# A second level of seven products inside an MLP's first matrix product, for two of the outer seven

## The chip, the cores and the metric

The kernel runs on one core of one Trainium2 chip. The metric is the device time of one execution in microseconds. Before the change three runs gave 2006.57, 2002.11 and 2002.98 us, so the median is 2002.98 us. All arithmetic is in float32: each product of two matrices is made of three passes over operands that are split into a high and a low part.

## The reference, cut to what matters

The network has two layers: attention and an MLP, then a gated linear recurrence and an MLP. The change concerns the first matrix of both MLPs, `h @ w_up`:

```
def sqrelu_mlp(h, w_up, w_down):
    return jnp.square(jax.nn.relu(h @ w_up)) @ w_down
...
    h = rmsnorm(x, mlp_norm[layer])              # x: 1024 tokens x 1024
    x = x + sqrelu_mlp(h, mlp_w_up[layer], mlp_w_down[layer])   # w_up: 1024 x 4096
```

## The kernel before, in words

The hidden layer is made transposed: 4096 rows (hidden features, in 32 blocks of 128) by 1024 columns (tokens). Row block `m` and row block `m + 16` are done together; the kernel calls that a pair (`pair`, line 643), and there are 16 of them in each layer. A pair is a 2x2 block product: two row blocks, two halves of the 1024 inner features, two halves of the tokens (512 each). It is done with seven block products in place of eight (Strassen-Winograd). The seven are numbered 1 to 7. Product 2 multiplies the upper row block's second half of the features (its right weight block, as it is stored) by those features of the first 512 tokens; product 4 multiplies the lower row block's right weight block by a combination of token blocks. The other five have sums of weight blocks or the left ones.

One product (`product`, line 623) has 128 rows, 512 inner features and 512 columns: four blocks of 128 features, and for each of them three matmuls of 512 columns (`mm3`, line 431: high by high, high by low, low by high). So a product is 12 matmuls, a pair is 84, and each matmul has its own load of a 128x128 weight.

Around the products a pair does this:

- four weight tiles of 256 KB are loaded (`raw`, tag `wr`); four sums `s1` to `s4` are made on VectorE (DVE, tag `m`); each of the seven weights is split (`weight_split`, line 450) into a high part (`wh`, a copy on ScalarE, ACT, or on DVE) and a low part (`wl`, a subtraction on DVE);
- the products gather in three PSUM banks: `main` (tag `q`: 1, 6, 7, 4 on top of each other), `side` (`q`: 5 and 3) and `own` (tag `p`: 2). `main` is copied out after 1, after 6 and after 7 (tag `t`); `own` and `side` are added on DVE;
- the four blocks of the hidden layer are squared after a ReLU on ACT, and they and three differences of them are stored to DRAM (7 stores of 256 KB, `d<-t`), for the MLP's second product (`down`), which loads them again.

Ahead of the pairs, `finish` (line 561) makes the token blocks of the seven products with their splits.

Nothing is issued in the order of the code. Every operation is recorded with a cost, its engine or engines and its buffers (`Schedule.add`), and a planner (`due`, `order`) then sets the order on each engine: work is ranked by when the matrix engine will want it, and among what is ready the lowest rank goes first. Buffers are given out tag by tag in the order of recording; there are 20 of `t`, 7 of `m`, 5 each of `wr`, `wh`, `wl`, 4 PSUM banks each of `p` and `q`. All loads and stores stand in one queue, that of SyncE (SP), in the planned order. Since one helper issues everything, every instruction stands under one line of the profile (L372), and groups are told apart by their tiles' names.

Of the kernel before, what the change touches and what calls it, by code (L numbers as in the profile page):

```python
# [22 lines left out]
NH = 2  # L23
TH = T // NH
FF = 4096
MT = FF // P
# [16 lines left out]
CH = 64  # L43
LEVELS = 6
WARM = 10
K_SPANS = ((-1, 3), (2, 6), (5, 8))


# [88 lines left out]
LEAD = 100  # L137
# [3 lines left out]
HK = KT // 2  # L141
# [167 lines left out]
def straight(z):  # L309

    return z.rearrange("p (b a) -> p a b", a=2)


def halves(z):

    return z.rearrange("p (a b) -> p a b", a=2)


class Net:
# [241 lines left out]
    def finish(self, which, r=None):  # L561

        x, t, q01, q11 = self.b, [], [], []

        def stored(j):
            z = self.t()
            self.dma(z, self.u[j], 4 * P * TH)
            return z

        def lower():  # L570
            for j in range(HK):
                q01.append(self.gained(which, j, 1, r))
# [24 lines left out]
        yield  # L597
        for j in range(HK):
            z = stored(j + HK)
            self.tt("any", z, z, t[j], ALU.subtract)  # L600
            x[4].append(self.split(z))
        yield

    def mlp_first(self, layer):
        self.layer, self.hid, self.y = layer, {}, {}
        self.begin(2 + layer)
        self.weigh(0)

    def mlp_second(self):
# [5 lines left out]
    def take(self, out, bank):  # L615

        self.copy(halves(out), straight(bank))
# [5 lines left out]
    def product(self, ps, w, x, start, n=TH):  # L623
        more = {} if start else {"skip_group_check": True}
        for j in range(HK):
            c = slice(j * P, j * P + P)
            self.mm3(ps, (w[0][:, c], w[1][:, c]), x[j], start and j == 0, j == HK - 1, n, **more)
# [12 lines left out]
        self.s.lead = 0  # L640
        return w

    def pair(self, m, x):

        w = self.strassen_weights(*(self.io["up"][self.layer, i] for i in (m, m + MT // 2)))

        def read(ps):
            z = self.t()
            self.take(z, ps)
            return z  # L650

        main, side, own = self.psum("q"), self.psum("q"), self.psum()
        got = {}
        for name in (1, 5, 6, 2, 7, 3, 4) if m == MT // 2 - 1 else (1, 2, 5, 6, 3, 7, 4):
            ps = main if name in (1, 6, 7, 4) else own if name == 2 else side
            self.product(ps, w[name], x[name], name in (1, 2, 5))
            if name in (1, 5, 6, 7):
                got[name] = read(ps)
        u1, p5, u2, u3 = (got[name] for name in (1, 5, 6, 7))

        def kept(name, z):
            self.hid[name, m] = self.keep(z)

        self.add_bank(u1, own)
        h00 = self.square_relu(u1)
        kept(1, h00)
        self.add_bank(u2, side)
        h01, t5, t6, t4 = self.square_relu(u2), *(self.t() for _ in range(3))
        self.tt("any", t5, h01, h00, ALU.subtract)
        kept(5, t5)  # L670
        self.tt("any", p5, p5, u3, ALU.add)
        h11 = self.square_relu(p5)
        kept(3, h11)
        self.tt("any", t6, h11, t5, ALU.subtract)
        kept(6, t6)
        self.tt("any", h01, h11, h01, ALU.subtract)
        kept(7, h01)
        h10 = self.square_relu(main, True)
        kept(2, h10)
        self.tt("any", t4, h10, t6, ALU.subtract)  # L680
        kept(4, t4)

    def mlp(self, cut):

        x = self.mlp_second()
        for m in range(MT // 2):
            if m == MT // 2 - 2:
                self.r = [self.a() for _ in range(NH)]
                for hf in range(NH):
                    self.copy(self.r[hf], self.spread(self.square[hf]))  # L690
            if m == 1 and self.layer == 0:
                self.hgrn_constants()
            self.pair(m, x)
        yield from self.down(cut)

    def hidden(self, name, p):
# [879 lines left out]
```

## Time and profile before

| | |
|---|---|
| median of three runs | 2002.98 us |
| the profiled execution | 2004.15 us |
| its span in the profile | 2002.0 us (2.15 us lie around it) |
| busy, share of the span: PE, weight loads, DVE, ACT | 99%, 86%, 85%, 51% |
| DMA | 345.88 MB, mean 173 GB/s |
| granted TensorE clock | full (0.998) |

PE stands for the matrix engine's matmuls, PEld for its weight loads. A matmul's row holds the time from its start to its modelled end, and the next one starts before that end; so the pace of the engine is read from the starts of following rows, not from the mean duration. The same holds for DVE to a smaller degree. The first products of the MLP run from about 295 to 583 us in the first layer and from about 1378 to 1668 us in the second.

### The profile page before, as it was taken

To read this page: it belongs to the slowest core of one execution; us is meant where nothing else is said; L and a number is where in the kernel's file an instruction comes from. 1 tells how busy PE (TensorE), PEld (TensorE's weight loads), DVE (VectorE), ACT (ScalarE), POOL (GpSimd) and SP (SyncE) were. 2 spreads that over 40 slices of the span, in tenths; PEclk is the share of its full clock that TensorE was granted. 3 is DMA by queue.
4 is the path that set the end of the run, shared out by engine and by line. 5 is a ranking of instruction groups with operands and counts; after the bars stand their busy time and mean duration, and the time that the engine had idled before them with its cause. 6 is when DMAs were issued, how large, how long until landed. Compare 5 with 4: busy or idle time off the path is not lost.

```text
span 2002.0 us, 32707 instructions
## 1 busy us (share of the span) xinstructions
PE 1979.2 (99%) x11404; PEld 1721.3 (86%) x11404; DVE 1700.5 (85%) x3360; ACT 1011.1 (51%) x2045; POOL 61.2 (3%) x124
## 2 busy tenths in 40 slices
PE   9999999999999999999999999999999999999998
PEld 8877788888888888888888888888888888888887
DVE  8999899777779878799888999889977778887787
ACT  6566796554444323255345555553654445333352
POOL 4030000000000000000000000000000000000001
PEclk9999999999999999999999999999999999999999
DMA  6211463544469877745412212667444447896752
GB/s 217 90 53 59 126 221 122 184 165 160 149 200 302 293 231 260 238 163 176 151 59 80 80 59 85 210 200 246 150 158 158 155 165 236 282 308 216 236 179 85
DMA packets 196677, 345.88 MB, mean 173 GB/s; under 512 B 21536, under 2 KB 31776, under 8 KB 196512
## 3 DMA queue, kind: packets, MB, share of 16 engines
q1 hardware_dynamic: 195936, 343.28, 52.3%
q8 instruction: 89, 1.46, 0.3%
q14 instruction: 76, 0.62, 0.1%
q10 hardware_dynamic: 576, 0.52, 0.1%
HBM read 250.39 MB, written 93.32 MB: 172 GB/s over the span
## 4 chain that ended last, share of the span: by engine, by line
PE 84%; DVE 8%; DMA 3%; issue 2%; ACT 2%; SPq 0%; POOL 0%; POOLq 0%; DVEq 0%; ACTq 0%
PE q L372 50%; PE p L372 33%; DVE t L372 3%; DVE a L372 2%; DVE wl L372 1%; DMA t<-d 1%; ACT t L372 1%; ACT a L372 1%; DMA wr<-in_down 1%; DVE m L372 0%; DMA a<-in_x 0%; ACT wh L372 0%; DMA wr<-in_wqkv 0%; ACT m L372 0%; DMA wr<-in_wv 0%
## 5 line engine op out<-in xcount | busy, mean ns | idle before, releaser
L372 PE MATMUL q<-a,wh 128*128 128x512 f32 x2560 | 762.3, 380 | 1.4 <-ACT t L372 1.4
L372 PE MATMUL p<-a,wh 128*128 128x512 f32 x2112 | 645.1, 384 | 0.1
L372 PEld LDWEIGHTS q<-a,wh 128*128 128x128 f32 x2560 | 483.5, 189 | 70.6 <-ACT t L372 2.5
L372 PE MATMUL q<-a,wl 128*128 128x512 f32 x1280 | 485.4, 380 | 0.0
L372 PEld LDWEIGHTS p<-a,wh 128*128 128x128 f32 x2112 | 395.0, 190 | 53.9 <-issue 1.2
L372 PE MATMUL p<-a,wl 128*128 128x512 f32 x1056 | 402.1, 381 | 0.0
L372 ACT CAST a<-t 128x512 fp32r<-128x512 f32 x277 | 168.4, 619 | 294.7 <-PE q L372 141.2
L372 PEld LDWEIGHTS q<-a,wl 128*128 128x128 f32 x1280 | 242.4, 189 | 33.8
L372 ACT ACTIVATE t<-t 128x512 f32<-128x512 f32 x272 | 171.1, 631 | 184.0 <-DVE t L372 175.3
L372 DVE TENSOR_TENSOR wl<-wr,wh 128x512 fp32r<-128x512 f32 x352 | 241.5, 689 | 12.4 <-ACT wh L372 3.9
L372 DVE TENSOR_TENSOR t<-t,t 128x512 f32<-128x512 f32 (+3 forms) x364 | 225.7, 642 | 26.8 <-ACT t L372 23.3
L372 PEld LDWEIGHTS p<-a,wl 128*128 128x128 f32 x1056 | 200.2, 190 | 26.5 <-issue 0.4
L372 DVE TENSOR_TENSOR a<-t,a 128x512 fp32r<-128x512 f32 (+1 forms) x326 | 217.3, 689 | 2.9 <-ACT a L372 2.4
L372 DVE TENSOR_TENSOR wl<-m,wh 128x512 fp32r<-128x512 f32 x248 | 170.9, 691 | 18.0 <-ACT wh L372 10.6
L372 ACT COPY t<-q 128x512 f32<-128x512 f32 (+2 forms) x214 | 119.2, 560 | 112.1 <-PE q L372 111.0
L372 ACT CAST wh<-wr 128x512 fp32r<-128x512 f32 x175 | 107.6, 618 | 93.7 <-PE p L372 41.6
L372 DVE TENSOR_TENSOR m<-wr,wr 128x512 f32<-128x512 f32 x160 | 110.3, 691 | 41.9 <-DMA wr<-in_down 25.9
L372 DVE CAST wh<-wr 128x512 fp32r<-128x512 f32 x177 | 75.8, 428 | 79.7 <-PE q L372 47.1
L372 ACT CAST wh<-m 128x512 fp32r<-128x512 f32 x158 | 97.3, 618 | 56.6 <-PE q L372 34.8
L372 PE MATMUL p<-wh,a 128*128 128x512 f32 x352 | 111.0, 385 | 0.0
L372 PEld LDWEIGHTS q<-t,t 128*64 128x64 f32 (+1 forms) x2160 | 95.2, 144 | 13.7 <-issue 5.6
L372 PE MATMUL q<-t,t 128*64 128x32 f32 (+2 forms) x2160 | 104.1, 229 | 1.6 <-DVE t L372 1.3
(130 smaller groups left out, 2059.9 us busy)
## 6 DMA issues: line engine op xcount, KB each, us to landing
d<-t SPq DMA_DIRECT2D x276, 256.0 KB, 2.8
t<-d SPq DMA_DIRECT2D x264, 256.0 KB, 4.6
wr<-in_down SPq DMA_DIRECT2D x256, 256.0 KB, 4.0
wr<-in_up SPq DMA_DIRECT2D x128, 256.0 KB, 2.9
a<-d SPq DMA_DIRECT2D x60, 256.0 KB, 4.8
wr<-in_wqkv SPq DMA_DIRECT2D x48, 256.0 KB, 2.9
d<-a SPq DMA_DIRECT2D x48, 256.0 KB, 3.5
wr<-in_win SPq DMA_DIRECT2D x48, 256.0 KB, 3.0
```

The source lines that it names most:

```text
L372: fn(*[place(a) for a in args], **{k: place(v) for k, v in kw.items()})
```

## The change

For the pairs from number 4 on (`m > AT` with `AT = 2`), the pairs are taken in couples of two neighbours, `m` and `m + 1`: six couples in each layer. For a couple, product 2 of both pairs and product 4 of both pairs are made together. The two upper right weight blocks, stacked, are 256 rows by 512 features, and the token block is 512 by 512; that is again a 2x2 block product, of quarters: 128 rows, 256 features, 256 columns. `inner` does it with seven products of six matmuls with 256 columns each. Pairs 0 to 3 of each layer keep the seven outer products as they were.

```
+INNER = (2, 4)
+AT = 2
...
+    def inner(self, name, m, x):
...
+        a0, a1 = (self.raw(self.io["up"][self.layer, i + row * (MT // 2)][:, TH:]) for i in (m, m + 1))
+        sa, sb = self.t(tag="m"), self.t(tag="m")
...
+        self.tt("any", s1, a1[:, near], a1[:, far], ALU.add, half)
+        self.tt("any", s2, s1, a0[:, near], ALU.subtract, half)
+        self.tt("any", s3, a0[:, near], a1[:, near], ALU.subtract, half)
+        self.tt("any", s4, a0[:, far], s2, ALU.subtract, half)
+        wide = [self.weight_split(z) for z in (a0, sa, sb)]
+        hi, lo = (self.tile(tag, BUFS[tag], (P, TH), F32R) for tag in ("wh", "wl"))
+        self.copy(hi[:, far], a1[:, far], half, ("ACT", "DVE"), False)
+        self.tt("any", lo[:, far], a1[:, far], hi[:, far].bitcast(F32), ALU.subtract, half)
...
+        banks = [self.psum(), self.psum()]
+        main, side, own = banks[0][:, near].only(0), banks[1][:, near].only(0), banks[1][:, far].only(1)
+
+        def product(k, ps, start):
...
+            if k in made:
+                right = [self.t(F32R) for _ in range(2)]
+                for z, kept in zip(right, made[k]):
+                    self.dma(z.bitcast(F32), kept, 4 * P * TH)
+            for i in range(2):
...
+                self.mm3(ps, (wh, wl), (xh, xl), start and i == 0, i == 1, half, slice(0, half), **more)
...
+        product(1, main, True)
+        take(part[0, 0], main)
+        product(2, own, True)
+        add(part[0, 0], own)
+        product(6, main, False)
+        take(part[0, 1], main)
+        product(5, side, True)
+        product(7, main, False)
+        take(part[1, 1], main)
+        add(part[1, 1], side)
+        product(3, side, False)
+        add(part[0, 1], side)
+        product(4, main, False)
+        take(part[1, 0], main)
```

The token side of the inner products 5, 6, 7 and 4 is made once in a layer, by `prepare`: differences of quarters of the stored token blocks, split and stored to DRAM as eight tiles of 256 KB for each of the two names. It is recorded between the outer products of pair 2. `inner` loads them again, two tiles for each of the four products.

```
+    def prepare(self, name):
...
+        u = [self.t() for _ in range(HK)]
+        for z, kept in zip(u, self.quarters[name]):
+            self.dma(z, kept, 4 * P * TH)
+        yield
...
+        def stored(k, t):
+            made[k] = [self.keep(z.bitcast(F32)) for z in self.split(t.rearrange("p i c -> p (i c)"), self.t)]
...
+        difference(t1, low(far), low(near))
+        stored(5, t1)
+        yield
...
```

In `pair` the weights of the products in `done` are not split (their raw tiles are still loaded, since `s1` and `s4` need them), the products are left out, and their results come from `inner`:

```
-        for name in (1, 5, 6, 2, 7, 3, 4) if m == MT // 2 - 1 else (1, 2, 5, 6, 3, 7, 4):
+            if name in done:
+                if name == 4:
+                    late = done[4]()
+                continue
...
+            if name == 1 and 2 in done:
+                self.add_bank(done[2], main)
...
-        h10 = self.square_relu(main, True)
+        if 4 in done:
+            self.tt("any", late, late, u3, ALU.add)
+            h10 = self.square_relu(late)
+        else:
+            h10 = self.square_relu(main, True)
```

How the instructions stand now is shown at three places of the first layer. On PE before, this is the start of product 2 of pair 7: its bank is `p1360`, the token blocks are `a814` and so on, and the weight is `wh1348`, `wl1349`.

```order
L372 MATMUL p1360_5419<-a814_3642,wh1348_5336 128x512
L372 MATMUL p1360_5419<-a815_3702,wh1348_5336 128x512
L372 MATMUL p1360_5419<-a814_3642,wl1349_5344 128x512
L372 MATMUL p1360_5419<-a818_3675,wh1348_5336 128x512
L372 MATMUL p1360_5419<-a819_3735,wh1348_5336 128x512
L372 MATMUL p1360_5419<-a818_3675,wl1349_5344 128x512
```

On PE now, this is inner product 6 of name 4 for the couple of pairs 6 and 7 (bank `p1438`), and the start of inner product 5 (bank `p1439`); `t1442` to `t1445` are prepared token quarters that were loaded again, and `q1482` is the `main` bank of pair 7.

```order
L374 MATMUL p1438_5584<-t1442_5647,wh1432_5582 128x256
L374 MATMUL p1438_5584<-t1443_5656,wh1432_5582 128x256
L374 MATMUL p1438_5584<-t1442_5647,wl1433_5602 128x256
L374 MATMUL p1438_5584<-t1442_5647,wh1432_5582 128x256
L374 MATMUL p1438_5584<-t1443_5656,wh1432_5582 128x256
L374 MATMUL p1438_5584<-t1442_5647,wl1433_5602 128x256
L374 MATMUL q1482_5675<-a798_3259,wl1473_5678 128x512
L374 MATMUL p1439_5588<-t1444_5682,wh1432_5582 128x256
L374 MATMUL q1482_5675<-a802_3624,wh1472_5667 128x512
L374 MATMUL q1482_5675<-a803_3658,wh1472_5667 128x512
L374 MATMUL q1482_5675<-a802_3624,wl1473_5678 128x512
L374 MATMUL p1439_5588<-t1445_5689,wh1432_5582 128x256
```

A product of twelve matmuls with 512 columns in one run has become runs of six with 256 columns, and outer products of the couple stand between them. In all, 1008 matmuls of 256 columns (24 inner blocks of 42) have taken the place of 576 of 512 columns (24 times two products of 12).

On the SP queue before, this is the stretch of one pair: four weight tiles (`wr<-in_up`) and seven stores (`d<-t`).

```order
L372 DMA wr1552_5988<-in_up 128x512
L372 DMA d14941495_5994<-t1494_5982 128x512
L372 DMA wr1553_6008<-in_up 128x512
L372 DMA wr1554_6052<-in_up 128x512
L372 DMA d14991500_6066<-t1497_6057 128x512
L372 DMA wr1594_6091<-in_up 128x512
L372 DMA d15011502_6098<-t1501_6080 128x512
L372 DMA d15021503_6109<-t1498_6095 128x512
L372 DMA d15031504_6121<-t1496_6046 128x512
L372 DMA d15051506_6133<-t1505_6107 128x512
L372 DMA d15061507_6141<-t1499_6127 128x512
```

On the SP queue now, this is the end of a pair's stores and the loads for the inner block of the PE rows above.

```order
L374 DMA d13771378_5627<-t1370_5614 128x512
L374 DMA wr1465_5636<-in_up 128x512
L374 DMA t1442_5647<-d11771178_4712 128x512
L374 DMA t1443_5656<-d11781179_4720 128x512
L374 DMA t1446_5664<-d11881189_4796 128x512
L374 DMA t1447_5673<-d11891190_4810 128x512
L374 DMA t1444_5682<-d11661167_4655 128x512
L374 DMA t1445_5689<-d11671168_4664 128x512
L374 DMA wr1501_5698<-in_up 128x512
L374 DMA wr1502_5709<-in_up 128x512
L374 DMA t1448_5722<-d11961197_4829 128x512
L374 DMA t1449_5730<-d11971198_4843 128x512
```

Eight loads of prepared tiles and two more weight tiles for each inner block now stand between the stores and loads of the pairs: for a couple, 42 transfers of 256 KB where there were 22.

On DVE now, this is the work for the weights of the same inner block (`m1428` and `m1429` hold the four sums, 256 columns each), between the additions of the pair before and the reading of inner banks (`p`). Before, none of the rows with 256 columns was there, and a right weight block needed only its split.

```order
L374 TENSOR_TENSOR m1428_5531<-wr1427_5484 128x256
L374 TENSOR_TENSOR m1429_5538<-wr1426_5474,wr1427_5484 128x256
L374 TENSOR_TENSOR t1393_5458<-p1392_5447,t1393_5458 128x256
L374 TENSOR_TENSOR wl1418_5550<-m1410_5414,wh1417_5528 128x512
L374 TENSOR_TENSOR wl1420_5556<-m1409_5409,wh1419_5542 128x512
L374 TENSOR_TENSOR m1428_5531<-m1428_5531,wr1426_5474 128x256
L374 TENSOR_TENSOR t1369_5572<-t1372_5494,t1368_5452 128x512
L374 TENSOR_TENSOR wl1431_5576<-wr1426_5474,wh1430_5563 128x512
L374 TENSOR_TENSOR m1429_5538<-wr1426_5474,m1428_5531 128x256
```

The sums and splits of an inner block now stand among the last additions of the pair ahead of it and the readings of the inner block before.

## Rows read from the trace of the kernel before

**Rows 1.** The page: span, engines' busy time, granted clock, chain by engine.
```profile
span 2002.0 us, 32707 instructions
PE 1979.2 (99%) x11404; PEld 1721.3 (86%) x11404; DVE 1700.5 (85%) x3360; ACT 1011.1 (51%) x2045; POOL 61.2 (3%) x124
...
PEclk9999999999999999999999999999999999999999
...
PE 84%; DVE 8%; DMA 3%; issue 2%; ACT 2%; SPq 0%; POOL 0%; POOLq 0%; DVEq 0%; ACTq 0%
```
**Rows 2.** The chain in order of time, first layer's pairs: start, length, what.
```profile
444.12 2.59 PE p L372 x12
446.71 15.54 PE q L372 x72
462.25 2.59 PE p L372 x12
```
**Rows 3.** Stages of the first products: busy time by engine, clock, DMA share, GB/s.
```profile
295.00:331.00 36.00, 35.41 (x168) 30.86 (x167) 35.62 (x62) 25.66 (x47) 0.36 (x2) 1.00 0.39 130
331.00:367.00 36.00, 36.00 (x169) 31.59 (x168) 34.07 (x89) 23.70 (x43) 0.00 (x0) 1.00 0.56 187
367.00:583.00 216.00, 216.00 (x1010) 189.33 (x1009) 156.51 (x261) 103.93 (x178) 0.00 (x0) 1.00 0.47 160
1378.00:1414.00 36.00, 36.00 (x172) 31.50 (x171) 34.90 (x61) 22.98 (x41) 0.00 (x0) 1.00 0.49 154
1414.00:1450.00 36.00, 36.00 (x168) 31.57 (x167) 34.25 (x63) 21.98 (x42) 0.00 (x0) 1.00 0.53 176
1450.00:1666.00 216.00, 216.00 (x1010) 189.37 (x1010) 158.23 (x263) 105.46 (x180) 0.00 (x0) 1.00 0.46 159
```
**Rows 4.** Timeline of PE and PEld near the end: 512 columns, then 256.
```profile
1954.63 0.38 PE L372 MATMUL p<-a,wl 128*128 128x512 f32 x1
...
1963.70 0.38 PE L372 MATMUL p<-a,wl 128*128 128x512 f32 x1
...
1970.93 9.23 PEld L372 LDWEIGHTS p<-a,a 128*128 128x128 f32 x82
1970.95 9.40 PE L372 MATMUL p<-a,a 128*128 128x256 f32 x82
```
**Rows 5.** The page's groups: weight loads of the first products.
```profile
L372 PEld LDWEIGHTS q<-a,wh 128*128 128x128 f32 x2560 | 483.5, 189 | 70.6 <-ACT t L372 2.5
```
**Rows 6.** Stages of the second product (down), columns as in Rows 3.
```profile
583.00:619.00 36.00, 34.63 (x161) 29.98 (x160) 31.09 (x54) 20.37 (x36) 0.00 (x0) 1.00 0.87 286
640.00:710.00 70.00, 70.00 (x326) 61.43 (x325) 59.16 (x107) 23.45 (x40) 0.00 (x0) 1.00 0.90 301
700.00:710.00 10.00, 10.00 (x48) 8.79 (x47) 9.27 (x19) 2.48 (x4) 0.00 (x0) 1.00 0.98 343
```
**Rows 7.** Timeline of DVE: runs of 512 and of 256 columns.
```profile
442.26 1.29 DVE L372 TENSOR_TENSOR t<-t,t 128x512 f32<-128x512 f32 x2
...
1028.70 2.90 DVE L372 TENSOR_TENSOR t<-t,m 128x256 f32<-128x256 f32 x8
```
**Rows 8.** Groups on DVE, 367 to 583 us: busy, mean ns, idle before.
```profile
L372 DVE TENSOR_TENSOR wl<-m,wh 128x512 fp32r<-128x512 f32 x48 | 33.2, 691 | 5.1 <-ACT wh L372 3.5
L372 DVE CAST wh<-wr 128x512 fp32r<-128x512 f32 x35 | 14.9, 427 | 19.6 <-PE q L372 13.7 <-PE p L372 5.7
```
**Rows 9.** Timeline of PE: the wait of the first pairs.
```profile
317.34 1.05 PE L372 MATMUL q<-c,t 128*128 128x1 f32 x8 [0.59 <-DVE t L372]
```
**Rows 10.** The page's DMA issues: count, KB, median us to landing.
```profile
d<-t SPq DMA_DIRECT2D x276, 256.0 KB, 2.8
t<-d SPq DMA_DIRECT2D x264, 256.0 KB, 4.6
wr<-in_up SPq DMA_DIRECT2D x128, 256.0 KB, 2.9
```

More of the change, by code (lines that the diff above doesn't have):

```diff
@@ L601, in finish @@
             x[4].append(self.split(z))
+            if r is None and 4 in INNER:
+                self.quarters[4].append(self.keep(z))
         yield
@@ L606, in mlp_first @@
         self.begin(2 + layer)
+        self.quarters = {2: self.u[HK:], 4: []}
         self.weigh(0)
@@ L641, in strassen_weights, with difference @@
         return w
-    def pair(self, m, x):
-        w = self.strassen_weights(*(self.io["up"][self.layer, i] for i in (m, m + MT // 2)))
+    def prepare(self, name):
+        near, far = slice(0, TH // 2), slice(TH // 2, TH)
+        u = [self.t() for _ in range(HK)]
+        for z, kept in zip(u, self.quarters[name]):
+            self.dma(z, kept, 4 * P * TH)
+        yield
+        made = self.quarters[name] = {}
+        def difference(out, x, y):
+            for i in range(2):
+                self.tt("any", out[:, i].only(i), x(i), y(i), ALU.subtract, TH // 2)
+        def stored(k, t):
+            made[k] = [self.keep(z.bitcast(F32)) for z in self.split(t.rearrange("p i c -> p (i c)"), self.t)]
+        low, high = (lambda c: lambda i: u[i][:, c]), (lambda c: lambda i: u[2 + i][:, c])
+        new = lambda: self.t(F32, (P, 2, TH // 2))
+        part = lambda t: lambda i: t[:, i].only(i)
+        t1 = new()
+        difference(t1, low(far), low(near))
+        stored(5, t1)
+        yield
+        t2 = new()
+        difference(t2, high(far), part(t1))
+        stored(6, t2)
+        yield
+        t3 = new()
+        difference(t3, high(far), low(far))
+        stored(7, t3)
+        yield
+        difference(t1, high(near), part(t2))
+        stored(4, t1)
+        yield
@@ L647, in read, with pair @@
+    def pair(self, m, x, done, between=()):
+        w = self.strassen_weights(*(self.io["up"][self.layer, i] for i in (m, m + MT // 2)), done)
         def read(ps):
@@ L650, in read @@
             return z
-        main, side, own = self.psum("q"), self.psum("q"), self.psum()
+        main, side, own = self.psum("q"), self.psum("q"), None if 2 in done else self.psum()
         got = {}
         for name in (1, 5, 6, 2, 7, 3, 4) if m == MT // 2 - 1 else (1, 2, 5, 6, 3, 7, 4):
+            if name in done:
+                if name == 4:
+                    late = done[4]()
+                continue
             ps = main if name in (1, 6, 7, 4) else own if name == 2 else side
             self.product(ps, w[name], x[name], name in (1, 2, 5))
-            if name in (1, 5, 6, 7):
+            if name == 1 and 2 in done:
+                self.add_bank(done[2], main)
+            elif name in (1, 5, 6, 7):
                 got[name] = read(ps)
-        u1, p5, u2, u3 = (got[name] for name in (1, 5, 6, 7))
+            for steps in between:
+                next(steps, None)
+        p5, u2, u3 = (got[name] for name in (5, 6, 7))
         def kept(name, z):
             self.hid[name, m] = self.keep(z)
-        self.add_bank(u1, own)
+        u1 = done[2] if 2 in done else got[1]
+        if 2 not in done:
+            self.add_bank(u1, own)
         h00 = self.square_relu(u1)
@@ L677, in pair @@
         kept(7, h01)
-        h10 = self.square_relu(main, True)
+        if 4 in done:
+            self.tt("any", late, late, u3, ALU.add)
+            h10 = self.square_relu(late)
+        else:
+            h10 = self.square_relu(main, True)
         kept(2, h10)
@@ L685, in mlp @@
         x = self.mlp_second()
[L686 to L693, printed above, removed]
+        steps = [self.prepare(name) for name in INNER]
+        for m in range(0, MT // 2, 2):
+            done = {}
+            if m > AT:
+                done = {name: self.inner_of(name, m, x) for name in INNER}
+            for i in range(2):
+                if m + i == MT // 2 - 2:
+                    self.r = [self.a() for _ in range(NH)]
+                    for hf in range(NH):
+                        self.copy(self.r[hf], self.spread(self.square[hf]))
+                if m + i == 1 and self.layer == 0:
+                    self.hgrn_constants()
+                self.pair(m + i, x, {name: y(i) if name == 2 else lambda y=y: y(i) for name, y in done.items()}, steps if m + i == AT else ())
         yield from self.down(cut)
```

30 lines of the change are left out of this document (added).

## The prediction

> **What bounds the kernel now.** I read the page's head first: PE is busy 99% of 2002.0 us, at the full clock in all 40 slices, and the chain that ended last lies on PE for 84% [rows 1]. Next, the chain inside the first layer's first products: 2.59 us of twelve matmuls in bank `p` (product 2), 15.54 us of seventy-two in `q` (the other six), then `p` again [rows 2]. So a pair takes 462.25 - 444.12 = 18.13 us, a couple 36.26 us, and the chain names nothing but PE there. Third, the stages of the first products: from 331 to 583 us and from 1378 to 1666 us PE is busy for the whole of each stretch; only the first 36 us lose 0.59 [rows 3], to one wait for DVE [rows 9]. DVE is nearly full in the first two couples of a layer (34.07 to 35.62 of 36 us) and has 26.1 us of work in each of the later six (156.51 / 6); ACT 17.3 us (103.93 / 6); DMA moves 160 GB/s at a share of 0.47. Here PE's matmuls set the time, one for one, and the question is what else becomes full when they get fewer.
>
> **The matmuls.** The pace is read from starts. With 512 columns, 14 rounds of three begin between 1954.63 and 1963.70: 9.07 / 42 = 0.216 us each. With 256 columns and a weight load for each matmul, as in `inner`, 82 loads take 9.23 us; less the last one's 0.19 [rows 5] that is 9.04 / 81 = 0.112 us each, and the matmuls beside them keep that pace (82 in 9.40 us) [rows 4]. Half the columns cost 52% of the time, not half: the load of 128 weight columns, hidden behind 512 columns, is just about the pace with 256. An inner block has 42 matmuls: 42 x 0.112 = 4.70 us. The two outer products that it replaces have 24: 24 x 0.216 = 5.18 us. It saves 0.48 us, and there are 2 names x 6 couples x 2 layers = 24 blocks: **-11.5 us**. A couple shrinks to 36.26 - 0.96 = 35.3 us.
>
> The Trainium skill speaks against this: "TensorE: Matmul & The Clock Gate", Part 3, "The mechanism", says that a weight load overlaps a running matmul only when the two use different row groups. All loads here use all 128 rows, so by that rule each of the 1008 loads would stand alone; at the 0.19 us of rows 5 the change would cost up to 1008 x 0.19 = 192 us. The rows disagree: 82 loads and 82 matmuls of 256 columns go by in the same 9.4 us [rows 4]. I leave that case out of the chances.
>
> **The vector work of a couple.** Four low parts are no longer made (products 2 and 4 of two pairs). The two inner blocks add six full low parts, eight sums and two low parts of 256 columns, six additions of 256 columns from PSUM; each pair adds `late + u3`. Net: 4 rows of 512 columns and 16 of 256. A DVE row of 512 follows the last after 1.29 - 0.69 = 0.60 us, one of 256 after about (2.90 - 0.44) / 7 = 0.35 us, with 0.44 as its own length [rows 7]: 2.4 + 5.6 = 8.0 us. The planned order has about 3 fewer casts on DVE in a couple (ACT takes them): -1.3 us at 0.43 [rows 8]. So DVE goes from 26.1 to 32.8 us of 35.3: 93%. ACT loses two copies and gets 7 casts and 8 half copies; even at 0.69 us each, as a full DVE row [rows 8], that is 10 us into 18 us of room.
>
> **The transfers of a couple.** 22 transfers of 0.262 MB become 42: 4 more weight tiles, 16 prepared tiles. That is 11.0 MB in 35.3 us, or 312 GB/s, twice the present rate. The stage that comes nearest is `down`: 70 us at 301 GB/s and a share of 0.90 with DVE at 59.16, and PE full for all 70; its best 10 us move 343 GB/s at 0.98 [rows 6]. So 312 GB/s fits, with 9% to spare, if the queue is never held up. At the 301 GB/s of those 70 us a couple would take 36.6 us, 1.3 more than PE: bounds 0 to 12 x 1.3 = 15.6 us. I take 0.2 us a couple, **+2.4 us**, much nearer to zero, because the nearest row (DVE 85%, DMA 90%, no PE loss) is nearly the state to come, and because the order puts outer products between the inner ones, so that a late load finds other matmuls ahead of it.
>
> The skill's "DMA: Bandwidth & Descriptors", "Specifications", has a ceiling of 435 GB/s for the SBUF side. By it the couple would use 72% of what there is, and the case of a full queue below could be dropped. Rows 6 do not agree: the engines are at 0.98 with 343 GB/s, so I keep it.
>
> **`prepare`, once in a layer.** For each name 8 differences of 256 columns and 4 low parts: 8 x 0.35 + 4 x 0.60 = 5.2 us of DVE, 10.4 for both, with 8 casts that ACT can take, and 28 transfers (8 loads, 16 stores, 4 more token blocks kept). It is recorded in pair 2, where DVE has 36 - 34.07 = 1.9 us free (second layer 1.75) [rows 3]. So some 8.6 us of other DVE work is pushed later. What is behind it: additions and differences of pairs 1 to 3 that end in stores, and the weights of pairs 3 and 4. The weights run pairs ahead of their products, the stores are not wanted for 200 us, and the couples after it have 2.5 us free each. Bounds: 0, or all 8.6 us on PE in each layer. The nearest row is the one with DVE at 35.62 of 36, which lost 0.59 [rows 3, 9]; I take 0.6 a layer: **+1.2 us**. The 28 transfers (7.3 MB beside 6.7 MB in that 36 us) do not fit into the couple and run into the next; what they delay is the first inner block's loads, which the same bound covers.
>
> **The change into `down`.** The first 36 us after the pairs lose 1.37 us in the first layer, with DMA at 286 GB/s [rows 6]. Its first weights now stand behind the last couple's loads, on a busier queue; or the order falls better. Bounds -1.4 to +1.4 us, taken as 0.
>
> **Sum.** -11.5 + 2.4 + 1.2 = -7.9 us against the profiled execution's 2004.15 us (span 2002.0): 1996.25. That execution is 1.17 us above the median of 2002.98; on the median's scale the forecast is **1995.1 us**.
>
> **Rivals.**
> 1. *The queue is the bound* (slower). All loads and stores stand in one queue; a store whose data are late holds the prepared loads behind it, and PE then waits at inner products 6, 5, 7 and 4. For: the rate doubles to 312 GB/s, loads of `t` already take 4.6 us to land against 2.8 for stores [rows 10]. Against: rows 6. It decides below 11.0 MB / 36.26 us = 304 GB/s, where a couple is as long as before; at 301: -11.5 + 15.6 + 1.2 = +5.3, so 2008.3 us.
> 2. *Weights late for the inner blocks* (no change). A split weight lasts PE 12 x 0.112 = 1.34 us in an inner block, 2.59 in an outer product, with the same five buffers; DVE has 4.6 us of work for 4.70 us of inner matmuls. For: DVE at 93%. Against: PE lost nothing at 34.90 of 36 [rows 3]. With a wait as in rows 9 once a couple, 12 x 0.59 = 7.1: 1999.8 us; at each of the 24 blocks: 2006.9 us.
> 3. *`prepare` does not hide* (slower): 17.2 in place of 1.2 us gives 2011.1 us. For: no room in that couple. Against: the weights' lead.
> 4. That the change does not do what it says is ruled out by the order: 1008 matmuls of 256 columns have replaced 576 of 512.
>
> **Chances.** Forecast 0.66, by itself 1990 to 1999 (with nothing lost and the gain at the change into `down`, 1990.1). Rival 2: 0.16; rival 1: 0.13; rival 3: 0.05. A difference under 0.2%, 4 us, cannot be told from none. Faster, below 1999.0: 0.66. Within 0.2%: rival 2 and 0.03 of rival 1, where it loses less than at 301 GB/s: 0.19. Slower: 0.10 + 0.05 = 0.15. The range 1990 to 2007 leaves out about 0.15 above and a little below.
>
> **What would show it.** Right: PE starts 0.112 us apart in runs of `p` with 256 columns; couples of 35.3 to 35.6 us; PE's idle time in 367 to 577 us under 2 us a layer; DVE at about 33 us and DMA near 310 GB/s in a couple. Rival 1 would show as waits of PE for loads `t<-d` and couples above 36.3 us; rival 2 as waits for `wh` and `wl` at each inner block; rival 3 as a gap before the first inner block. Wrong altogether: couples no shorter, or a pace above 0.123 us (5.18 / 42), at which nothing is saved.

## The result, and the profile after

The changed kernel takes 2010.65 us (median of 8 runs, 2009.55 to 2014.02), the kernel before, run beside it, 2005.08 us (8 runs, 2002.11 to 2008.81). The ratio is 1.0029 with a 95% interval of 1.0019 to 1.0039: slower by 5.8 us by that ratio, where 7.9 us less were forecast.

The page's head after the change, against [rows 1], and the chain by engine:

```profile
span 2009.2 us, 34678 instructions
PE 1977.0 (98%) x11836; PEld 1721.9 (86%) x11836; DVE 1779.3 (89%) x3589; ACT 1087.6 (54%) x2240; POOL 62.2 (3%) x124
...
PEclk9999999999999999999999999999999999999999
...
PE 73%; DVE 12%; DMA 7%; issue 3%; ACT 3%; SPq 1%; POOL 0%; POOLq 0%; DVEq 0%; ACTq 0%
```

PE still seems full, but the chain that ended last lies on it for 73% in place of 84%; DVE and DMA have taken the rest. The stages of the first products, with the columns of [rows 3], show where:

```profile
331.00:367.00 36.00, 36.00 (x169) 31.52 (x167) 35.93 (x96) 23.53 (x43) 0.00 (x0) 1.00 0.76 255
367.00:403.00 36.00, 35.99 (x191) 31.85 (x190) 31.98 (x64) 23.88 (x46) 0.00 (x0) 1.00 0.96 334
...
367.00:583.00 216.00, 212.77 (x1198) 189.22 (x1197) 189.79 (x364) 133.65 (x258) 0.00 (x0) 1.00 0.89 307
1450.00:1666.00 216.00, 212.50 (x1183) 188.34 (x1181) 188.74 (x358) 134.33 (x258) 0.00 (x0) 1.00 0.89 305
```

The stretch with `prepare` (331 to 367 us) lost nothing, with DVE at 35.93 of 36. The couples lost 3.2 and 3.5 us of PE's busy time in 216 us. That is not all: a busy matmul's modelled end hides short waits, so the starts must be read. The timeline of PE, in an inner product 5 of the first layer's second couple:

```profile
426.82 0.38 PE L374 MATMUL q<-a,wh 128*128 128x512 f32 x1
427.04 0.38 PE L374 MATMUL q<-a,wl 128*128 128x512 f32 x1
427.25 0.38 PE L374 MATMUL p<-t,wh 128*128 128x256 f32 x2
427.99 0.35 PE L374 MATMUL p<-t,wh 128*128 128x256 f32 x1 [0.35 <-DMA t<-d]
428.18 0.28 PE L374 MATMUL p<-t,wl 128*128 128x256 f32 x1
428.29 0.28 PE L374 MATMUL p<-t,wh 128*128 128x256 f32 x1
```

The pace is as forecast: 0.22 us after a matmul of 512 columns, 0.11 after one of 256. The second of the two matmuls that begin at 427.25 starts 0.112 us later, at 427.36; the third, at 427.99, comes 0.63 after it, so this step lost 0.52 us, although the row calls only 0.35 of it idle. The next step, 0.18 us, lost another 0.07. I add up all such losses (step less 0.216 or 0.112, from 0.03 us on) in 380 to 600 and 1465 to 1700 us and call the sum of both layers *lost steps*. Before: 0.75 us. After: 8.06 + 9.15 = 17.2 us. So -11.5 + (17.2 - 0.75) = +5.0 us of the measured +5.8 are accounted for. By what the profile names at the end of a step, the largest sums go to loads of prepared tiles (`t<-d`: 3.3 and 4.2 us); by place, 10.9 us lie at the matmuls of inner product 5.

The two stretches are fixed in time, so in a run whose couples end earlier or later they take in, or miss, a wait of the change into `down`. Where two runs are compared I therefore also give the sum from the first to the last matmul of the inner blocks in each layer, and say *within the couples*: 16.7 us here.

The chain into the wait at 427.99, in order of time (start, length, what), goes from DVE through a store and a load to PE:

```profile
417.09 1.22 DVE t L374 x2
418.30 0.02 issue
418.32 3.37 DMA d<-t
421.69 0.02 issue
421.70 0.02 SPq L374
...
422.19 5.66 DMA t<-d
427.86 0.14 issue
427.99 0.35 PE p L374
```

A difference on DVE ends at 418.30; its store goes out at once and lands at 421.69. The chain names this landing as what the SP queue waited for, to load into the `t` buffer that the store had read; the load that PE needs is issued at 422.19, behind that one, and lands 5.66 us later. The page's transfers against [rows 10]: each kind lands later, the weights most.

```profile
t<-d SPq DMA_DIRECT2D x472, 256.0 KB, 4.9
d<-t SPq DMA_DIRECT2D x316, 256.0 KB, 3.5
...
wr<-in_up SPq DMA_DIRECT2D x176, 256.0 KB, 4.3
```

### The profile page after: what moved, and what is told of

Its sections match the earlier page's. It is cut to its first block, busy times and chain, and to the rows that moved or that the text cites. A ratio compares the mean times of both kernels' runs of the same rounds, so it can differ in the third digit from the quotient of the medians.

```text
span 2009.2 us, 34678 instructions
## 1 busy us (share of the span) xinstructions
PE 1977.0 (98%) x11836; PEld 1721.9 (86%) x11836; DVE 1779.3 (89%) x3589; ACT 1087.6 (54%) x2240; POOL 62.2 (3%) x124
## 4 chain that ended last, share of the span: by engine, by line
PE 73%; DVE 12%; DMA 7%; issue 3%; ACT 3%; SPq 1%; POOL 0%; POOLq 0%; DVEq 0%; ACTq 0%
PE q L374 40%; PE p L374 33%; DVE t L374 5%; DMA t<-d 3%; DVE wl L374 3%; DVE a L374 2%; DVE m L374 1%; ACT t L374 1%; DMA d<-t 1%; SPq L374 1%; DMA wr<-in_down 1%; ACT wh L374 1%; ACT a L374 0%; DMA a<-in_x 0%; DMA wr<-in_wv 0%
## 5 line engine op out<-in xcount | busy, mean ns | idle before, releaser
L374 PE MATMUL q<-a,wh 128*128 128x512 f32 x2368 | 710.1, 380 | 2.1 <-DVE t L374 1.3
L374 PE MATMUL p<-a,wh 128*128 128x512 f32 (+1 forms) x2208 | 640.1, 370 | 0.7 <-ACT t L374 0.4
L374 PEld LDWEIGHTS q<-a,wh 128*128 128x128 f32 x2368 | 442.7, 189 | 64.5 <-ACT t L374 2.4
L374 PE MATMUL q<-a,wl 128*128 128x512 f32 x1184 | 448.4, 379 | 0.0
L374 PE MATMUL p<-a,wl 128*128 128x512 f32 (+1 forms) x1104 | 404.6, 367 | 0.2 <-DVE wl L374 0.2
L374 DVE TENSOR_TENSOR t<-t,t 128x512 f32<-128x512 f32 (+3 forms) x428 | 259.0, 629 | 26.5 <-ACT t L374 22.7
L374 DVE TENSOR_TENSOR wl<-wr,wh 128x512 fp32r<-128x512 f32 (+1 forms) x352 | 233.9, 667 | 11.9 <-ACT wh L374 4.7
L374 ACT CAST wh<-wr 128x512 fp32r<-128x512 f32 (+1 forms) x234 | 140.3, 601 | 155.0 <-PE q L374 62.8
L374 ACT COPY t<-q 128x512 f32<-128x512 f32 (+3 forms) x190 | 105.3, 557 | 65.5 <-PE q L374 64.2
L374 DVE CAST wh<-wr 128x512 fp32r<-128x512 f32 (+1 forms) x118 | 49.5, 420 | 43.5 <-PE q L374 22.7
```

Source lines behind the costliest of these rows:

```text
L374: fn(*[place(a) for a in args], **{k: place(v) for k, v in kw.items()})
```

## The experiments

The theory at the start was that the prepared loads are late. The rivals were `prepare` itself, DVE at nearly full load, and the rate of the DMA engines. Each ratio below is against the kernel before, run on the same chip, with its 95% interval.

**`prepare` alone** (e4): no couple uses `inner`, everything else stays.

```
-            if m > AT:
+            if m > MT:
```


> prepare runs in both layers, but no couple uses what it made: all 16 pairs keep their seven outer products. This prices the step alone. My term of 0.6 us a layer gives ratio 1.0006; the case in which the work does not hide (8.6 us a layer) gives 1.0086.

Measured: 0.9999 (0.999 to 1.0008), lost steps 1.3 us. `prepare` costs nothing that can be measured.

**No prepared loads** (e1): products 5, 6, 7, 4 read resident token blocks (so products 2 and 4 of these pairs get other values).

```
             if k in made:
-                right = [self.t(F32R) for _ in range(2)]
-                for z, kept in zip(right, made[k]):
-                    self.dma(z.bitcast(F32), kept, 4 * P * TH)
+                right = x[name][k % HK]
```


> Leaves out the loads of the prepared token quarters: inner products 6, 5, 7 and 4 take token blocks that lie in SBUF instead (so their values are other ones); prepare itself still runs. 16 transfers fewer in a couple, 26 in place of 42, and 16 fewer uses of the t buffers. Theory 'the transfers hold PE' (the prepared loads come late): the 16 us of waits at inner products go, about 11.5 us of the matmuls' gain stay, ratio to the kernel before 0.994 to 0.997. Theory 'weights late' (DVE at 90% of a couple): the waits stay, ratio 1.001 or more.

Measured: 1.0000 (0.9991 to 1.0008); lost steps 4.6 + 5.7 = 10.4 us, all within the couples, with DMA at 203 GB/s. So without the loads 6.3 of the 16.7 us within the couples go, and most of the loss is still there. What is left has one place: 6.6 us lie at product 5, and in the first layer there are twelve lost steps, one for each inner block, that DVE's `t<-p,t` ends. The timeline of PE and DVE at the longest of them:

```profile
496.98 0.68 DVE L374 TENSOR_TENSOR t<-t,t 128x512 f32<-128x512 f32 x1
...
497.13 0.28 PE L374 MATMUL p<-a,wl 128*128 128x256 f32 x1
497.58 0.41 DVE L374 TENSOR_TENSOR t<-p,t 128x256 f32<-128x256 f32 x1
...
498.05 0.38 PE L374 MATMUL p<-a,wl 128*128 128x256 f32 x1 [0.64 <-DVE t L374]
```

In the built program the matmul at 497.13 is the last of product 6, the one at 498.05 the third of product 5. DVE adds `own` (product 2) from its bank until 497.99, behind two other operations. Product 5 doesn't need that sum, and its weight and tokens are long there (product 6 has just used the same weight tile). But it writes `side`, the other half of the same PSUM bank (`banks[1]`). The plan takes the halves for independent (`.only(0)`, `.only(1)`); in the built program the first matmul of product 5 that stands behind the addition in the plan waits for it. The Trainium skill says in "PSUM — Partial Sum Buffer", "Terms", that the compiler keeps two engines from one bank of the same partitions at a time; the trace agrees, with 0.81 us lost at this place (0.92 for a step of 0.11).

**A bank of its own for `own`**, with all loads (e5) and without the prepared loads (e11):

```
-        banks = [self.psum(), self.psum()]
-        main, side, own = banks[0][:, near].only(0), banks[1][:, near].only(0), banks[1][:, far].only(1)
+        main, side, own = (self.psum()[:, near].only(0) for _ in range(3))
```


> Product 2 of each inner block (`own`) gets a PSUM buffer of its own; all loads stay. Theory A (two causes): without any prepared load the couples still waited 4.6 and 5.7 us a layer, nearly all at the first matmul of inner product 5, for the vector engine's addition of `own`. The plan takes the two halves of one PSUM buffer for independent, the built program makes product 5 wait for whoever reads the other half. With a buffer of its own that wait goes: PE's excess over 0.216/0.112 us steps falls from 8.1 and 9.2 us a layer to about 4, the ratio to before goes from 1.003 to 0.998 to 0.9995. Rival B (the vector engine is simply late at 93%): the same additions are awaited one product later (3 or 6), the excess stays at 8 to 9 us, the ratio at 1.002 to 1.004. Rival C (three buffers of four for one block): the next block's product 1 waits for buffers, and the ratio rises above 1.004.

> No prepared tile is loaded (products 6, 5, 7 and 4 of the inner blocks read resident token blocks, so products 2 and 4 of these pairs are not the right ones), and `own` has a PSUM buffer of its own: against the first experiment only the buffer changes. Theory A: the vector engine's wait at product 5 (3.0 us a layer, nearly all of what was left there) goes, excess 10.4 -> 4 us or less over both layers, ratio 0.996 to 0.997. Rival B: the same additions are awaited at products 3 and 7, excess 8 us or more, ratio 0.998 to 1.000.

Measured: e5 1.0017 (1.0009 to 1.0026), lost steps 13.8 us, 12.2 within the couples; e11 0.9957 (0.9945 to 0.997), lost steps 3.9 us, 2.6 within the couples. Of the difference in e5, 0.95 us are one wait in the change into `down`, which begins at 1699.7 us; in the changed kernel the like wait begins behind 1700. In e5 no step within the couples is lost to `t<-p,t` any more, but loads are still awaited at product 5 (`t<-d`: 2.1 and 3.5 us), and the ratio stays above the 0.998 to 0.9995 that theory A gave. With both causes gone, the kernel gains 8.6 us. The stages of e11:

```profile
367.00:583.00 216.00, 215.26 (x1225) 194.15 (x1225) 196.59 (x375) 136.06 (x261) 0.00 (x0) 1.00 0.59 206
1450.00:1666.00 216.00, 215.46 (x1226) 193.75 (x1225) 194.90 (x371) 136.62 (x263) 0.00 (x0) 1.00 0.60 208
```

DVE has more work in them than before in this stretch (196.6 us of 216), and PE's busy time loses under 1 us: a DVE at 91% does not cost much by itself. The two causes cover each other. Within the couples, removing the bank's wait is worth 4.4 us of lost steps with the loads and 7.8 without; removing the loads is worth 6.3 us with the shared bank and 9.7 with its own. By the ratios it is 2.4 and 8.6 us for the bank, 5.8 and 12.0 for the loads; the 2.4 alone is not clear of noise, since the intervals of e5 and the changed kernel overlap.

**Half of each load**, with the shared bank (e2) and with its own (e6); the same number of transfers in the same order, 128 KB for each prepared tile (both feature blocks then read the same half, so the values are other ones):

```
-                    self.dma(z.bitcast(F32), kept, 4 * P * TH)
+                    self.dma(z[:, :half].bitcast(F32), kept[:, :half], 4 * P * TH)
...
-                    xh, xl = (z[:, i * half : (i + 1) * half] for z in right)
+                    xh, xl = (z[:, :half] for z in right)
```


> The same transfers in the same order on every engine, but each prepared load moves half of its tile (128 KB in place of 256 KB), and both feature blocks use that half (values are other ones). Bytes of a couple go from 11.0 to 8.9 MB, 252 GB/s. Theory 'the DMA engines are full': the waits go, ratio 0.995 to 0.997. Theory 'the one queue is held': loads are issued as late as before behind stores whose data are late, only their landing is shorter; more than half of the 16 us of waits stay, ratio 0.999 to 1.002.

> As the run with the own PSUM buffer, and each prepared load moves only half of its tile (128 KB; both blocks of a product then read the same columns, so products 2 and 4 of these pairs are not the right ones). Theory A: both causes are gone; the excess is under 2 us a layer, the ratio 0.994 to 0.9965 (-11.6 us of matmuls plus up to 4). Rival B: the excess stays at 4 to 6 us as with half loads alone, the ratio at 0.998 to 0.999.

Measured: e2 0.9985 (0.9976 to 0.9994), between the ranges of its two theories, lost steps 9.6 us; e6 0.9965 (0.9953 to 0.9977), 7.4 us (5.9 within the couples), none of them at product 5. The transfers of e2 in 367 to 583 us, then those of the changed kernel there:

```profile
d<-t SPq DMA_DIRECT2D x93, 256.0 KB, 3.3
wr<-in_up SPq DMA_DIRECT2D x71, 256.0 KB, 3.8
t<-d SPq DMA_DIRECT2D x96, 128.0 KB, 3.6
```
```profile
d<-t SPq DMA_DIRECT2D x94, 256.0 KB, 3.6
t<-d SPq DMA_DIRECT2D x89, 256.0 KB, 5.2
wr<-in_up SPq DMA_DIRECT2D x70, 256.0 KB, 4.7
```

With the same buffers and the same order on the queue a load lands 1.6 us sooner after its issue, and PE's waits for `t<-d` are gone. But the queue itself also stands still less. In the built program 1416 of the 1614 transfers of SP's queue carry a wait for the landing of the eighth transfer before them. What SP waited for, from 385 to 600 us (us in total, times, longest), first in the changed kernel, then in e2:

```profile
SPq L374 <- DMA t<-d: 15.5, 42, 1.3
```
```profile
SPq L374 <- DMA t<-d: 2.4, 2, 1.9
```

In the kernel before, SP waited for no landing of such a load there; in e6 neither. So halving the loads takes away both their late landing and SP's waits for it, and e2 and e6 do not separate the two. They do show that the loads' size matters: 8.8 us by the ratios with the shared bank, 10.4 with its own.

**Less for DVE** (e12): as e6, and two of the four low parts of an inner block are not made (their high parts stand in).

```
-        wide = [self.weight_split(z) for z in (a0, sa, sb)]
+        wide = [self.weight_split(a0)]
+        for z in (sa, sb):
+            hi = self.tile("wh", BUFS["wh"], (P, TH), F32R)
+            self.copy(hi, z, TH, ("ACT", "DVE"), False)
+            wide.append((hi, hi))
```


> As the run with the own PSUM buffer and half loads, and the low parts of two of the four split weight tiles of an inner block are not made (their high part stands in, so products 2 and 4 of these pairs are not the right ones): 8 rows of 0.60 us less on the vector engine in a couple, 4.8 us, 31.5 -> about 27 of 36 us; matmuls and loads as there. Theory (what is left, 7.4 us over both layers, comes from vector and scalar work that ends just late at 90% load): excess under 4 us, ratio 0.994 to 0.9955. Rival (what is left is the latency from PE to the copy and back to PE, whatever the load): excess 6 to 8 us, ratio 0.996 to 0.997.

Measured: 0.9956 (0.9942 to 0.9969), lost steps 2.9 us. The expectation had miscounted: a couple loses 4 such rows, not 8 (70 rows `wl<-m` in e6's first layer, 47 here), and DVE did 182.12 us of 216 in place of 191.42. Even so, half of e6's lost steps within the couples go (5.9 to 2.9 us); those of e6 for which the profile names a cause are waits for vector and scalar work. Against e6 the intervals overlap (e6 0.9953 to 0.9977), so the gain in time is not shown.

**Another queue** (e3): the prepared loads are issued by GpSimd.

```
-                    self.dma(z.bitcast(F32), kept, 4 * P * TH)
+                    self.dma(z.bitcast(F32), kept, 4 * P * TH, "Pool")
```


> The prepared loads are issued from GpSimd's queue, which is idle in this stage, with everything else left in SP's; bytes and buffers are the same. Theory 'the one queue is held': loads no longer stand behind stores and start as soon as a t buffer is free; most of the waits go, ratio 0.995 to 0.999. Theory 'the DMA engines are full': 42 transfers of 256 KB as before, ratio 1.002 to 1.004. Theory 'the t buffers are short': the loads wait for the stores that free their buffers, ratio 1.001 to 1.004 too, and the two would have to be told apart by the landing times.

Measured: 1.0447 (1.0427 to 1.0467), lost steps 82 us (93 within the couples, which last to 634 and 1765 us here). What GpSimd and DVE waited for from 400 to 600 us, and the stage:

```profile
POOL t L374 <- PE p L374: 102.1, 13, 20.7
DVE m L374 <- DMA wr<-in_up: 37.7, 15, 4.6
```
```profile
367.00:583.00 216.00, 192.84 (x1011) 171.72 (x1011) 161.90 (x309) 114.81 (x219) 43.07 (x80) 0.94 0.78 270
```

The loads wait for a buffer that PE is still reading. But among the causes of PE's waits the profile names no prepared load. From 385 to 600 us PE waits for DVE's `t` (13.0 us), ACT's `t` (8.8) and one `wl` (2.8), and DVE itself waits 37.7 us for raw weights (2.7 in the changed kernel). One such place, on DVE and on PE:

```profile
563.96 0.43 DVE L374 TENSOR_TENSOR m<-wr 128x256 f32<-128x256 f32 x1 [4.60 <-DMA wr<-in_up]
...
566.45 0.41 DVE L374 TENSOR_TENSOR t<-p,t 128x256 f32<-128x256 f32 x1
...
566.92 0.38 PE L374 MATMUL p<-t,wl 128*128 128x256 f32 x1 [3.85 <-DVE t L374]
```

DVE comes late to the addition of `own` because it waited for weights, and product 5 waits for that addition over the shared bank: 35.9 of the 82 us are steps of product 5 that DVE's `t` ends. So e3 does not price a queue for the loads; the same change with the bank of e5 was not run. After waits of up to 4 us the granted clock fell to a mean of 0.94 (of its two levels 2.4 GHz reads as 1.00). "DMA: Bandwidth & Descriptors" of the Trainium skill, "Issuing engines are not separate DMA queues", says that another issuing engine saves only the time to issue; no run here shows a gain from one. What of the loss is the clock's, and why the weights came late (the plan counts each queue as if it had the DMA engines to itself), was not separated.

**An earlier place in the plan** (e7): as e5, and 5000 ns in place of 2000 for the landing of a prepared load.

```
-                    self.dma(z.bitcast(F32), kept, 4 * P * TH)
+                    self.dma(z.bitcast(F32), kept, 4 * P * TH, tail=5000.0)
```


> As the run with the own PSUM buffer, and the plan counts 5000 ns instead of 2000 ns for the landing of a prepared load (the after-trace: 4.9 us), so that it orders them earlier on the queue. Theory A with loads issued too late by plan: a further 2 to 4 us a layer of waits for t<-d goes; ratio 0.995 to 0.998. Rival D (a prepared load can't be issued before one of the 20 `t` buffers is free, and stands behind stores in the same queue): no gain over the run with the own buffer alone, or a loss of up to 5 us, since buffers are held longer.

Measured: 1.0038 (1.0026 to 1.005), lost steps 20.5 us. The waits for `t<-d` shrank from 5.6 us in e5 to 1.3, and `t<-p,t` (5.1 us) and `wl` (3.6 us) took their place, at products 3 and 1 above all. That the earlier loads hold buffers and stand ahead of weights fits this; it was not tested by itself.

**One name only** (e8): as e5, `INNER = (2,)`.

> As the run with the own PSUM buffer, but only product 2 by inner products: 32 transfers in a couple instead of 42 (8.4 MB in 35.8 us, 235 GB/s), half of the saving (-5.8 us). If the amount of transfers is what costs (half loads cost nothing), waits are about 1 us a layer and the ratio is 0.9975 to 0.999, equal to or better than with both products. If waits come from the inner blocks themselves, about 2.5 us a layer, ratio 0.999 to 1.000.

Measured: 1.0047 (1.0031 to 1.0063), lost steps 12.2 us; a miss. The stage and the loads in it:

```profile
367.00:583.00 216.00, 213.07 (x1103) 187.17 (x1102) 166.07 (x298) 117.19 (x220) 0.00 (x0) 1.00 0.69 236
```
```profile
t<-d SPq DMA_DIRECT2D x48, 256.0 KB, 5.2
```

DMA is down to 236 GB/s at a share of 0.69, no step waits for `t<-d`, and yet 6 us a layer are lost, now to `wl` (2.3 and 1.4 us), additions and copies. So a lower rate alone does not bring the gain; which waits come up depends on the order that the plan finds. The loads land 5.2 us after their issue here too, but early enough: from 384 to 590 us the tightest lands 4.1 us before its first matmul (median 7.8), against 0.04 us (median 1.5) in the changed kernel and 0.6 (median 3.1) in e2. 3.8 us of its loss lie outside the couples, unexplained.

**A version with fewer loads** (e9, e10), with the bank of e5. From pair 4 on nobody reads the far halves of the first two token blocks of names 2 and 4; the tiles of product 5 just fit there and are loaded once a layer. e10 also counts 3500 ns of landing.

```
-            if k in made:
+            if k in made and k != 5:
...
-                    xh, xl = (z[:, at] for z in x[name][i if k == 1 else 2 + i])
+                    xh, xl = (z[:, at] for z in x[name][i if k in (1, 5) else 2 + i])
...
+                if m + i == AT + 1:
+                    for name in INNER:
+                        for j in range(2):
+                            for z, kept in zip(x[name][j], self.quarters[name][5]):
+                                self.dma(z[:, TH // 2 :].bitcast(F32), kept[:, j * TH // 2 : (j + 1) * TH // 2], 2 * P * TH)
```


> As the run with the own PSUM buffer; and the token blocks of inner product 5 stay in SBUF: once pair 3 is done, the far halves of the first two token blocks of products 2 and 4 are read by nobody, and the prepared tiles of product 5 are loaded into them once a layer. Prepared loads of a couple fall from 16 to 12 (42 to 38 transfers, 10.0 MB in 35.3 us = 282 GB/s), and product 5, at which nearly all waits for loads lie, needs none. The result is the full one. Theory A (shared bank, and prepared loads too late for product 5): nearer to the run with half loads and own bank (0.9965) than to the one with the own bank alone (1.0017): ratio 0.9965 to 0.9985, excess 4 to 5 us a layer, none of it at product 5. Rival D (a late load is simply awaited one product later, at 7): ratio 1.000 to 1.002, excess 6 to 8 us a layer.

> As the run before, and the plan counts 3500 ns for the landing of a prepared load in place of 2000 (5000 made the waits move from loads to buffers and weights). Loads late by plan: ratio 0.001 below the run before it. Buffers held longer: 0.001 to 0.003 above it.

Measured: e9 0.9992 (0.9984 to 1.0001), lost steps 12.6 us, 1.7 of them for `t<-d`; e10 1.0001 (0.9992 to 1.001), 9.9 us. With both changes of e9 the +5.8 us become -1.6 (-3.2 to +0.2), but the rival was half right: the waits moved to products 6, 7 and 3. Within the couples e9 loses as much as e5 (12.1 and 12.2 us), so the 5.0 us between them are not explained by these steps.

**Buffers** (e14, e15, e13, e16): as e9 with 21 of `t` and 6 of `m`, and with 22 and 5; as e5 with 18 of `t`; and the kernel before with 18 of `t`.

```
-BUFS = {"a": 58, "t": 20, "m": 7, "sm": 8, "wr": 5, "wh": 5, "wl": 5, "p": 4, "q": 4}
+BUFS = {"a": 58, "t": 21, "m": 6, "sm": 8, "wr": 5, "wh": 5, "wl": 5, "p": 4, "q": 4}
```


> As the run with product 5 resident (0.9992), with 21 buffers of `t` and 6 of `m` in place of 20 and 7 (SBUF holds no more of both). Theory E: one buffer more of `t` brings 0.0005 to 0.002, ratio 0.997 to 0.9987, unless the sums of the weights then wait for `m`. Rival F: no change, 0.9985 to 1.000.

> As the run with product 5 resident and 21 `t`, with 22 of `t` and 5 of `m`. If `t` is what is short: ratio 0.9965 to 0.998, below the 0.9981 of 21. If the sums of weights now wait for `m` (an outer pair takes four of the five, an inner block two): above 0.9985.

> As the run with the own PSUM buffer (1.0017), with 18 buffers of tag `t` in place of 20; every instruction and transfer is the same, only when a buffer comes free changes. Theory E (a prepared load is late because it has to wait for one of the `t` buffers, which a store frees only when it has landed): two buffers fewer cost clearly, ratio 1.004 or more, excess 18 us or more over both layers. Rival F (only the queue and the landing time count, the buffers are not short): ratio within 0.001 of 1.0017.

> The kernel before, with 18 buffers of `t` in place of 20: the control for the run with 18 buffers after the change, which lost 0.0074 against 20 (only 3.8 us of about 15 within the couples). If that loss belongs to the changed kernel's need of `t`: ratio 1.000 to 1.002. If `t` is as short in the kernel before (attention, `down`, recurrence): 1.004 to 1.008, and the couples' share is the 3.8 us alone.

Measured: e14 0.9981 (0.9973 to 0.999), lost steps 11.5 us; e15 1.0004 (0.9995 to 1.0012), 9.9 us; e13 1.0091 (1.0075 to 1.0106), 17.6 us; e16 1.0082 (1.0068 to 1.0096), 1.0 us. The control decides e13: the kernel before loses as much, and all of it outside the stretches of the couples, so most of e13's loss does not belong to the change. Within the couples e13 loses 19.0 us where e5 loses 12.2, so 6.8 us do; the 3.8 us named in the last expectation leave out e13's first wait, which begins at 378.7 us, ahead of the fixed stretch. That two buffers fewer are felt in the couples fits the chain above; that the buffers are the cause of the late loads is not shown. e15 loses fewer steps than e14 and is still slower, so here too part of the time lies elsewhere. e14 is faster than both kernels: 3.8 us under the kernel before (5.4 to 2.0), and so some 9.6 under the changed one, by their ratios. It is the fastest measured of the versions that keep every product, though its interval overlaps that of e9. Its stages:

```profile
367.00:583.00 216.00, 215.12 (x1220) 193.29 (x1219) 189.56 (x361) 138.59 (x268) 0.00 (x0) 1.00 0.85 290
1450.00:1666.00 216.00, 212.32 (x1202) 190.03 (x1201) 190.94 (x370) 132.54 (x253) 0.00 (x0) 1.00 0.84 288
```

PE's busy time still loses 3.7 us in the second layer; the longest waits there are for copies on ACT (2.0 us).

How far the measure carries: -11.5 us (e8: half of it) plus the lost steps above those of before comes within 3.2 us of the measured difference in every run with inner blocks but e3 (couples longer than the stretches, and the clock), e8 (3.8 us off) and e13 (see the control).

## Why the prediction was wrong, step by step

- *What bounds*: right. PE's matmuls set the time one for one, which is why each lost step shows.
- *The matmuls, -11.5 us*: right. Steps of 0.112 us stand in the trace, also where 256 and 512 columns alternate; e11 and e12, with little else lost, gain 8.6 and 8.8 us. The 192 us that the prediction works out from the Trainium skill's rule on weight loads did not come.
- *The vector work*, 32.8 us a couple: 189.79 / 6 = 31.6 in 36 us. *The transfers*, 312 GB/s: 307 at a share of 0.89. Both are near enough.
- *The couples' waits, +2.4 us*: this step failed. It was 16.4 us, 1.4 a couple and a little over the upper bound of 15.6. The value was taken from a stage with the same shares ("nearly the state to come"). The shares were right and the inference was wrong, for two reasons. A share says how much is moved, not when. The prepared loads are issued behind waits of SP for buffers and for earlier landings, and land 5.2 us after their issue; the median lands 1.5 us before its first matmul, and the outer products between the inner ones did not cover the late ones at product 5. Taking the loads away is worth 6.3 us within the couples, or 9.7 without the shared bank. Which of buffers, landing and the waits for earlier landings makes them late stays open. And the bank that `own` and `side` share stood in the quoted code, but no term, bound or rival spoke of it; alone (without loads) it costs 7.8 us.
- *`prepare`, +1.2 us*: nothing (e4: -2.0 to +1.6). From 331 to 367 us DVE is now busy for 35.93 of 36 us and PE lost nothing, so the price of [rows 9] was not that of a full DVE.
- *The change into `down`, 0*: the one long wait there costs a step 0.84 us in the first layer, where before it cost 1.53, and 0.80 in the second, where before it cost 0.25; together that is near zero, within the ±1.4.
- *Rivals.* Rival 1 gave nearly the right time (+5.3 us, measured +5.8), and its sign, PE's waits for `t<-d`, was there. That the sum fits is partly luck: it puts the whole loss down to the transfers, while without any prepared load 10.4 us of steps are still lost. Its rate, under 304 GB/s, proves nothing either way: the bytes of a couple are fixed, so the measured rate (307 GB/s at a share of 0.89) only restates how long a couple takes. e8 shows that a rate of 236 GB/s does not bring the gain by itself. Rival 2's waits for `wh` and `wl` took about 1.5 us. Rival 3 did not happen.

## What to carry to other kernels

Where a plan cuts a buffer into parts, check in the built program that the hardware's unit (here a PSUM bank) is cut as well; such a wait is small at each place, and over 24 inner blocks it was worth 4 to 8 us of lost steps. An operand that is fetched again for each use is judged by the chain store, free buffer, load, landing, first use, and not by the rate alone: a stage with the same DMA share (`down`, 0.90) lost nothing in 70 us, this one did. And when one engine is full and two others are near it, read lost time from the starts of its instructions: 17 us were lost under a busy share that fell from 99% to 98%.

## What the runs showed of the hardware

A wait costs PE more than its length. In the changed kernel's second layer 23 steps, most of them right behind a wait, lost 2.2 us although the profile names nothing that they waited for, some 0.1 us each. The timeline at such a place:

```profile
555.97 0.19 PEld L374 LDWEIGHTS p<-t,wh 128*128 128x128 f32 x1 [0.70 <-DVE t L374]
555.97 0.38 PE L374 MATMUL p<-t,wh 128*128 128x256 f32 x1 [0.51 <-DVE t L374]
556.08 0.19 PEld L374 LDWEIGHTS p<-t,wl 128*128 128x128 f32 x1
556.18 0.28 PE L374 MATMUL p<-t,wl 128*128 128x256 f32 x1
```

Elsewhere a weight load runs ahead of its matmul, beside the one before. Here the load began only with its matmul; the next load starts 0.11 us behind the matmul, and the next matmul comes 0.21 us after it in place of 0.112.

For stores and raw weights the time to land grew with the traffic. From 367 to 583 us a store of 256 KB (`d<-t`) landed 2.8 us after its issue at a DMA share of 0.47 (before), 3.1 at 0.69 (e8) and 3.6 at 0.89 (after); a raw weight tile (`wr<-in_up`) in 2.9, 3.2 and 4.7 us. A prepared tile took 5.2 us both at 0.69 and at 0.89, the half of it 3.6 us at 0.77 (e2).
